# Weight halves issued in one piece, a regrouped chain, a third weight buffer and shared key tiles in a two-layer hybrid block

## The chip, the cores and the metric

The kernel runs on one core of one Trainium2 chip. The metric is the device time of one execution in microseconds (us). Engines: PE is TensorE (PEld its weight loads), DVE VectorE, ACT ScalarE, POOL GpSimd, SP SyncE. Each engine takes its instructions strictly in its own order.

## The reference

Two layers over 256 context tokens and 512 latent tokens (768 in all), model width 1024. Layer 0 keeps all 768 tokens, layer 1 gives only the 512 latent ones. All matrix products are fp32; the kernel splits each operand in two parts (hi and lo) and adds three products.

```python
# per layer: adaLN modulation, then the mixer
zc, zl = hc @ w_in, hl @ w_in          # one input projection, split into:
# A  bidirectional RWKV-7: 16 heads of 64, per token and direction
#    S = S*w - (S kk) (kk*a)^T + v k^T ;  y = S r ;  then group norm, bonus, gate
# B  GLU -> depthwise conv of width 31 -> LayerNorm -> silu
# C  grouped attention (8 query heads, 2 key heads), qk-RMSNorm, axial rotary
out = (sum_i gate_i * (branch_i @ w_branch_i)) @ w_out
x = x + mod * rms_norm(out)
# then the MLP, width 4096
x = x + mod * rms_norm(square(relu(h @ w1)) @ w2)
```

The scan of branch A is computed in chunks of 64 tokens: 12 chunks for each of two directions.

## The kernel before

**Phases.** Each layer runs rwkv_phase (branch A, the input projection and the conv; about 112 to 1370 us in layer 0, 2510 to 3690 us in layer 1), merge_phase (attention, branch products, output product) and mlp_phase (64 products by `gemm`, L389, with nothing between them).

**Pairs.** rwkv_phase goes over eight pairs of heads. One turn of the loop works on pair p and prepares pair p+1, and a generator weaver (`weave`) puts the pieces side by side. In the order of PE a turn has three stages, and this document calls them A, G and S:

- **A**, from the merge to the bonus. Of pair p: `rw_merge` (L892, its scaled copies on ACT at L900, L904), `rw_batch` (L920, L931; DVE L932, L934), then `rw_chain`, 12 steps that carry the state S (L952 and L956 give the next state, ACT scales it at L958, L968 and L970 add up the output y). Of pair p+1: the shifted inputs k, r, v (DVE L658), `rw_kk` (PE sums L717, L700, DVE L726), `rw_decay`, `rw_keys`. Of pair p-1: the readout.
- **G**, from the bonus (L877) to the last gram: `rw_grams`, twelve times eight or four small products (L810), masked by DVE (L814) and transposed by PE (L819).
- **S**, the solve: 30 DVE steps on small tiles (L861, L862) with two transposes at its end (L863, L864), small products L845 and L743, until the next merge.

**Big products.** The input projection is not a phase of its own. `job` queues products of eight k-steps; `fill(n)` takes n k-steps from the queue and issues their matmuls at L412. A k-step is three products (hi x hi, hi x lo, lo x hi), each in two pieces of 384 columns in layer 0 (one of 512 in layer 1). Four k-steps share one weight half: 24 matmuls in layer 0, 12 in layer 1. `pe(us)` calls `fill` in proportion to the small work just issued. Weight halves come by DMA, are split by ACT (`wh`, L328) and POOL (`wl`, L330) or DVE, and sit in two buffers. The 31 conv taps of each pair are DVE instructions (L473) put between the others in the same way.

**What sets the order.** Issue order gives each instruction a priority; the tile framework then orders every engine by its own estimate of when operands are ready. So a big matmul issued in one place can be moved between small ones on PE. Under `tc.high_priority()` an instruction goes ahead of those without it.

**Memory.** `KM` (values) and `BK` (keys) are separate tiles per direction; `KM` is read by L920 in A, `BK` written by `rw_keys` of the next pair in A and read by the grams in G.

Of the kernel before, what the change touches and what calls it, by code (L numbers as in the profile page):

```python
# [18 lines left out]
D = 1024  # L19
# [57 lines left out]
class Kern:  # L77
# [451 lines left out]
    def att_stats(s, T, hold):  # L529

        nc = s.nc
        rs = s.ars = s.cp.tile([128, 2, 10, 6], F32, tag="ars", name="ars", bufs=1)
        slots = []
        for n in (('BK', 0), ('BK', 1), ('KM', 0), ('KM', 1), ('GL', 0)):
            t = s.big[n]
            t = t.rearrange({3: "p a b -> p (a b)", 4: "p a b c -> p (a b c)", 5: "p a b c d -> p (a b c d)"}[len(t.shape)])
# [110 lines left out]
    def stage(s):  # L647
        return s.wp.tile([128, TOK], F32, tag="f0", name="f0", bufs=1)
# [60 lines left out]
    def rw_kk(s, P, p, I):  # L709
# [6 lines left out]
        for t in range(6):  # L716
            nc.tensor.matmul(sp[:, t, :], lhsT=sq[:, t * 128:t * 128 + 128], rhs=s.bo[:, 0:128:64], start=True, stop=True)  # L717
# [20 lines left out]
    def rw_transpose(s, src, h, dst):  # L738
# [3 lines left out]
        for m in range(6):  # L742
            nc.tensor.transpose(out=vp[:, m, :], in_=src[ROWS[h], m * 128:m * 128 + 128], identity=s.ident[ROWS[h], 64 * h:64 * h + 64])  # L743
# [45 lines left out]
    def rw_front(s, I, Q, d, g, lat):  # L789
# [18 lines left out]
        for q in range(4):  # L808
            for h in range(2):
                nc.tensor.matmul(gp[h][:, q, 0:n, :], lhsT=BK[ROWS[h], 4 * g + q].rearrange("p a b -> p (a b)"),  # L810
                                 rhs=KR[ROWS[h], 0:n, 4 * g + q, :], start=True, stop=True)
# [6 lines left out]
        for q in range(4):  # L818
            nc.tensor.transpose(out=bk[:, q].rearrange("p a b -> p (a b)"), in_=BK[:, 4 * g + q].rearrange("p a b -> p (a b)"), identity=s.ident)  # L819
# [16 lines left out]
    def rw_rest(s, d):  # L836
# [3 lines left out]
        for g, m in ((0, 8), (8, 4)):  # L840
            mv = s.g([128, 8, 64])
            for c in range(g, g + m):
                for h in range(2):
                    w = ROWS[1 - h]
                    nc.tensor.matmul(mv[ROWS[h], c - g, :], lhsT=GL[w, h, c, :], rhs=UV[w, h * 12 + c, :], start=True, stop=True)  # L845
# [20 lines left out]
    def rw_bonus(s, P, p, I, Q, T):  # L866
# [8 lines left out]
        for b, t0, t1 in s.pieces(T):  # L875
            bp = s.g([128, t1 - t0])
            nc.tensor.matmul(bp, lhsT=s.bo, rhs=ks[:, t0:t1], start=True, stop=True)  # L877
# [5 lines left out]
    def rw_merge(s, Q, d):  # L883

        nc = s.nc
# [4 lines left out]
        for q in range(12):  # L890
            for h in range(2):
                nc.tensor.matmul(xp[two[h], q, :], lhsT=GL[one[h], h, q, c:c + 32], rhs=Dn[one[h], q, :], start=True, stop=True)  # L892
        TT = Q['TT', d] = GL.rearrange("p h c t -> p (h c t)")[:, 0:768].rearrange("p (c t) -> p c t", t=64)
        Xn = Dn
        for h in range(2):
            nc.scalar.activation(out=Xn[two[h]], in_=xp[two[h]], func=AF.Copy, scale=-1.0)
        yield 1.1 + s.sched['merge']
        for h in range(2):
            for o, m in ((0, s.tlo), (32, s.thi)):
                nc.scalar.activation(out=TT[ROWS[h], :, o:o + 32], in_=Dt[ROWS[h]], func=AF.Copy, scale=m[ROWS[h]])  # L900
        tr = s.g([128, 12, 32])
# [7 lines left out]
    def rw_batch(s, Q, d, lat):  # L909
# [27 lines left out]
    def rw_chain(s, Q, lat, note, free):  # L937
# [5 lines left out]
        for k in range(NCH):  # L943
            q = (k, ORD_B[k])
            need_y = not lat or k >= 4
            seg = 0 if k < 4 else 1
            if k < NCH - 1:
                sp = s.pc.tile([128, 2, 64], F32, tag="c", name="sp")
                Sn = t("S", [128, 2, 64], 2)
                for d in range(2):  # L950
                    for h in range(2):
                        nc.tensor.matmul(sp[ROWS[h], d], lhsT=GB[d][:, h, q[d], 0, :], rhs=UV[d][:, h * 12 + q[d], :], start=d == 0, stop=d == 1 and k == 0)  # L952
                if k:
                    for d in range(2):
                        for h in range(2):
                            nc.tensor.matmul(sp[ROWS[h], d], lhsT=KR[d][ROWS[h], 0, q[d], :], rhs=S[ROWS[h], d], start=False, stop=d == 1)  # L956
                for d in range(2):
                    nc.scalar.activation(out=Sn[:, d], in_=sp[:, d], func=AF.Copy, scale=Q['lam', d][:, q[d]:q[d] + 1])  # L958
            if need_y:
                fresh = seg not in yp  # L960
                if fresh:
                    yp[seg] = s.py.tile([128, 512], F32, tag="y", name="yp")
                for part in ((1, 0) if k else (0,)):
                    for d in range(2):
                        o = (q[d] - 4 * seg) * 64
                        for h in range(2):
                            if part:
                                nc.tensor.matmul(yp[seg][ROWS[h], o:o + 64], lhsT=KR[d][ROWS[h], 1, q[d], :], rhs=S[ROWS[h], d], start=fresh, stop=False)  # L968
                            else:
                                nc.tensor.matmul(yp[seg][ROWS[h], o:o + 64], lhsT=GB[d][:, h, q[d], 1, :], rhs=UV[d][:, h * 12 + q[d], :], start=fresh, stop=d == 1 and k in (3, NCH - 1))  # L970
                        fresh = False
# [10 lines left out]
    def rw_readout(s, l, P, p, Q, T, dst):  # L982
# [144 lines left out]
    def rwkv_phase(s, l, P, T):  # L1127
# [3 lines left out]
        with ExitStack() as rc:  # L1131
# [7 lines left out]
            for a, b in lay[3]:  # L1139
# [7 lines left out]
                ('GB', [128, 2, 12, 2, 64]), ('UV', [128, 24, 64]), ('KM', [128, 12, 2, 64]))}  # L1147
# [47 lines left out]
            for p in range(8):  # L1195
# [21 lines left out]
                if more:  # L1217
                    gs.append(chain(prep(p + 1, In, Qn, *held), wait('s3'), grams(In, Qn, 0), wait('s7'), grams(In, Qn, 1), wait('s11'), grams(In, Qn, 2)))
# [16 lines left out]
            s.pin = False  # L1235
# [99 lines left out]
    def mlp_phase(s, l, PP, T, acc, actx):  # L1335
# [15 lines left out]
        with tc.tile_pool(name="mlp", bufs=1) as sp:  # L1351
# [29 lines left out]
            s.R = s.rstd(sp, ss, T, 1.0 / D, 0, CTX)  # L1381
# [65 lines left out]
```

## Time and profile before

| | us |
|---|---|
| time, median of three runs | 4514.72 (4509.4 to 4517.8) |
| the profiled execution | 4503.07, span 4501.3 |
| PE busy | 4197.0 (93%) |
| PEld busy | 3411.4 (76%) |
| DVE busy | 2642.9 (59%) |
| ACT busy | 1889.5 (42%) |
| POOL busy | 831.3 (18%) |
| mean granted clock | 0.956 of full speed |

The profiled execution is 11.65 us below the median. The busy time of PE counts a matmul until its modelled end, so matmuls that follow each other overlap in it; how long one really takes is read from the starts of its neighbours. A granted clock of 1.00 is 2.4 GHz, 0.50 is 1.2 GHz.

Stage times of a steady pair, read from the starts of L892, L877 and the end of the last L810. Pair 4 of layer 0: A 819.5 to 901.4, G to 922.5, S to 966.7. Pair 2 of layer 1: A 2953.0 to 3021.4, G to 3043.2, S to 3078.9. Sums over the seven pairs that prepare a next one: layer 0 A 543.7, G 151.8, S 324.1 us; layer 1 A 478.1, G 150.4, S 304.3 us.

### The profile page before, as it was taken

The page shows a single profiled execution, that of the slowest core. Times are in us where ns is not written, and L with a number is a line of the kernel's source. Part 1 is how long each engine was busy: PE and PEld are TensorE (multiplying, and loading weights), DVE is VectorE, ACT ScalarE, POOL GpSimd, SP SyncE. Part 2 cuts the span into 40 slices and gives each one's busy share as a digit, 9 for nine tenths or more (in the row PEclk, how much of TensorE's full clock was granted, in tenths as well). Part 3 has the DMA queues.
Part 4 walks back from the last instruction along what each step waited for, and adds up shares of the span by engine and source line. Part 5 has one row for each costly group of instructions (what it writes and reads, how often), then busy time and mean ns, then how long its engine had stood idle before and what let it go on. Part 6 is the DMA issues. An engine that isn't in the chain of part 4 may idle for free. (4 is left out here: it accounts for less than half of the span.)

```text
span 4501.3 us, 76922 instructions
## 1 busy us (share of the span) xinstructions
PE 4197.0 (93%) x31232; PEld 3411.4 (76%) x31232; DVE 2642.9 (59%) x4762; ACT 1889.5 (42%) x3690; POOL 831.3 (18%) x737
## 2 busy tenths in 40 slices
PE   6999999999998989899999899999999988898998
PEld 4888888888786668689999667877777775475886
DVE  3788788887855443132233568778787845443344
ACT  3455445444534442232223354555555534434333
POOL 0011221212112144300000102122122212262001
PEclk8999999999999999999999889999999979998998
DMA  4211111111224234343322221111111223142332
GB/s 161 62 47 53 57 58 57 51 52 58 73 84 157 71 110 142 126 141 117 107 87 63 69 61 52 50 60 47 56 54 57 75 71 121 57 133 64 96 96 82
DMA packets 438346, 364.05 MB, mean 81 GB/s; under 512 B 19022, under 2 KB 386792, under 8 KB 431848
## 3 DMA queue, kind: packets, MB, share of 16 engines
q1 hardware_dynamic: 417256, 279.43, 20.5%
q10 hardware_dynamic: 20736, 79.70, 4.9%
q8 instruction: 247, 4.05, 0.4%
q14 instruction: 107, 0.88, 0.1%
HBM read 299.29 MB, written 53.48 MB: 78 GB/s over the span
## 5 line engine op out<-in xcount | busy, mean ns | idle before, releaser
L328 ACT ACTIVATE wh<-raw 128x512 fp32r<-128x512 f32 x700 | 441.4, 631 | 1261.5 <-PE mm L389 558.3
L330 POOL TENSOR_TENSOR wl<-raw,wh 128x512 fp32r<-128x512 f32 x388 | 535.5, 1381 | 2062.3 <-ACT wh L328 1699.1
L412 PE MATMUL mm<-hh,wh 128*128 128x384 f32 (+1 forms) x2072 | 668.6, 381 | 49.4 <-ACT wh L328 40.7
L412 PE MATMUL mm<-hl,wh 128*128 128x384 f32 (+1 forms) x2072 | 644.5, 370 | 7.0 <-POOL hl L330 7.0
L412 PE MATMUL mm<-hh,wl 128*128 128x384 f32 (+1 forms) x2072 | 641.4, 369 | 4.9 <-POOL wl L330 4.6
L332 DVE TENSOR_TENSOR wl<-raw,wh 128x512 fp32r<-128x512 f32 x312 | 215.5, 691 | 589.7 <-ACT wh L328 586.4
L412 PEld LDWEIGHTS mm<-hh,wh 128*128 128x128 f32 x2072 | 379.2, 195 | 112.7 <-ACT wh L328 45.6
L473 DVE SCALAR_TENSOR_TENSOR cv<-u,dw,cv 128x783 f32<-128x783 f32 (+1 forms) x480 | 458.3, 955 | 3.1
L412 PEld LDWEIGHTS mm<-hl,wh 128*128 128x128 f32 x2072 | 389.6, 195 | 47.7 <-issue 12.1
L412 PEld LDWEIGHTS mm<-hh,wl 128*128 128x128 f32 x2072 | 388.0, 194 | 47.1 <-POOL wl L330 10.8
L412 PE MATMUL mm<-oh,wh 128*128 128x384 f32 (+1 forms) x768 | 256.7, 389 | 12.1 <-DVE acc L1273 4.1
L412 PE MATMUL mm<-oh,wl 128*128 128x384 f32 (+1 forms) x768 | 245.9, 374 | 22.0 <-POOL wl L330 22.0
L412 PE MATMUL mm<-ol,wh 128*128 128x384 f32 (+1 forms) x768 | 243.5, 370 | 6.6 <-POOL ol L330 5.6
L389 PE MATMUL mm<-hh,wh 128*128 128x384 f32 (+1 forms) x768 | 239.3, 367 | 6.3 <-ACT hh L347 3.6
L389 PE MATMUL mm<-hl,wh 128*128 128x384 f32 (+1 forms) x768 | 238.3, 365 | 5.5 <-POOL hl L330 5.0
L389 PE MATMUL mm<-hh,wl 128*128 128x384 f32 (+1 forms) x768 | 236.0, 362 | 0.0
L389 PE MATMUL mm<-fh,wh 128*128 128x384 f32 (+1 forms) x768 | 230.2, 353 | 0.0
L389 PE MATMUL mm<-fh,wl 128*128 128x384 f32 (+1 forms) x768 | 230.0, 353 | 0.0
L389 PE MATMUL mm<-fl,wh 128*128 128x384 f32 (+1 forms) x768 | 229.8, 353 | 0.0
L862 DVE TENSOR_TENSOR A<-A,Z 128x30 f32<-128x30 f32 (+14 forms) x480 | 198.2, 413 | 15.8
L861 DVE TENSOR_TENSOR Z<-A 128x30 f32<-128x30 f32 (+14 forms) x480 | 190.7, 397 | 16.5
L412 PEld LDWEIGHTS mm<-oh,wh 128*128 128x128 f32 x768 | 143.9, 195 | 55.2 <-ACT wh L328 15.8
(294 smaller groups left out, 7425.6 us busy)
## 6 DMA issues: line engine op xcount, KB each, us to landing
raw<-in_w_in_dram SPq DMA_DIRECT2D x316, 256.0 KB
raw<-in_w_ff_dram SPq DMA_DIRECT2D x256, 256.0 KB
wmod<-in_w_mod_dram ACTq DMA_DIRECT2D x48, 1024.0 KB
raw<-in_w_branch_dram SPq DMA_DIRECT2D x96, 256.0 KB
z<-f ACTq DMA_DIRECT2D x40, 384.0 KB
gt<-z SPq DMA_DIRECT2D x24, 384.0 KB
raw<-in_w_out_dram SPq DMA_DIRECT2D x32, 256.0 KB
z<-f ACTq DMA_DIRECT2D x32, 256.0 KB
```

What stands on the lines that cost most here:

```text
L328: nc.scalar.activation(out=hi, in_=src, func=AF.Copy)
L330: nc.gpsimd.tensor_tensor(out=lo, in0=src, in1=hi.bitcast(F32), op=ALU.subtract)
L332: nc.vector.tensor_tensor(out=lo, in0=src, in1=hi.bitcast(F32), op=ALU.subtract)
L389: nc.tensor.matmul(ps[:, b, :t1 - t0], lhsT=w[:, k % 4, :], rhs=a[:, t0:t1], start=k == 0 and f == 0, stop=k == KT - 1 and f == 2)
L412: ins = nc.tensor.matmul(s.jps[:, b, :t1 - t0], lhsT=w[:, k % 4, :], rhs=a[:, t0:t1], start=k == 0 and f == 0, stop=k == KT - 1 and f == 2)
L473: s.tap_pin(nc.vector.scalar_tensor_tensor(out=hold['c'], in0=u[:, k:k + L], scalar=w(k), in1=hold['c'], op0=ALU.mult, op1=ALU.add))
L861: nc.vector.tensor_tensor(out=tm, in0=X[:, k + 1:, k:k + 1].to_broadcast([128, n, k]), in1=X[:, k:k + 1, 0:k].to_broadcast([128, n, k]), o ...
L862: nc.vector.tensor_tensor(out=X[:, k + 1:, 0:k], in0=X[:, k + 1:, 0:k], in1=tm, op=ALU.add)
```

## The change

- **`fill`**: of the 24 (or 12) matmuls of a weight half all but the first are issued at high priority. A branch that never ran (`s.pin`) goes.
- **Buffers**: three weight halves in place of two, and `fill` asks for halves two ahead. The stage tile f0 of the input products gets two buffers.
- **Keys**: `KM` becomes another name for `BK`. `rw_keys` of the next pair now waits in the weaver for the batch of this pair (`b0`, `b1`). The attention's scratch slots move accordingly.
- **Merge**: the scaled copies move from ACT (four instructions on 64 rows) to DVE (two on 128 rows), per direction. The two evictions on ACT get an order-only dependency on the last weight split that was issued.
- **Chain**: y's first part (GB x UV) leads, then both parts of the state, its eviction, then y's second part.

```diff
+    def keep(s, first):
+        return nullcontext() if first else s.tc.high_priority()
...
-                while s.halves and len(s.ready) < 2:
+                while s.halves and len(s.ready) < s.nw:
...
-                    ins = nc.tensor.matmul(s.jps[:, b, :t1 - t0], lhsT=w[:, k % 4, :], rhs=a[:, t0:t1], start=k == 0 and f == 0, stop=k == KT - 1 and f == 2)
-                    if s.pin and f == 0 and b == 0:
-                        s.tc.keep_in_program_order(ins)
+                    with s.keep(k % 4 == 0 and f == 0 and b == 0):
+                        nc.tensor.matmul(s.jps[:, b, :t1 - t0], lhsT=w[:, k % 4, :], rhs=a[:, t0:t1], start=k == 0 and f == 0, stop=k == KT - 1 and f == 2)
...
-        return s.wp.tile([128, TOK], F32, tag="f0", name="f0", bufs=1)
+        return s.wp.tile([128, TOK], F32, tag="f0", name="f0", bufs=2)
...
         for h in range(2):
-            nc.scalar.activation(out=Xn[two[h]], in_=xp[two[h]], func=AF.Copy, scale=-1.0)
+            ins = nc.scalar.activation(out=Xn[two[h]], in_=xp[two[h]], func=AF.Copy, scale=-1.0)
+            s.tc.add_manual_dep(ins.ins, hi.ins.name, mybir.DependencyInfo(mybir.DependencyClass.NoSync, mybir.DependencyReason.DATA), reason="weights first")
...
-        for h in range(2):
-            for o, m in ((0, s.tlo), (32, s.thi)):
-                nc.scalar.activation(out=TT[ROWS[h], :, o:o + 32], in_=Dt[ROWS[h]], func=AF.Copy, scale=m[ROWS[h]])
+        for o, m in ((0, s.tlo), (32, s.thi)):
+            nc.vector.tensor_scalar(out=TT[:, :, o:o + 32], in0=Dt, scalar1=m, scalar2=None, op0=ALU.mult)
...
-        s.nraw, s.nw, s.lo_pool, s.turn = 2, 2, False, 0
+        s.nraw, s.nw, s.lo_pool, s.turn = 2, 3, False, 0
...
+            s.big.update({('KM', d): s.big['BK', d] for d in range(2)})
...
-                return chain(s.after(I, 'k', 0, s.rw_kk(P, p, I)), *held, s.rw_decay(P, p, Q), s.rw_keys(P, p, I, Q, 0), s.rw_keys(P, p, I, Q, 1),
+                return chain(s.after(I, 'k', 0, s.rw_kk(P, p, I)), *held, s.rw_decay(P, p, Q), wait('b0'), s.rw_keys(P, p, I, Q, 0), wait('b1'), s.rw_keys(P, p, I, Q, 1),
```

What the instruction order shows. Over the whole program the matmuls of L412 stand in 975 unbroken runs before and 386 runs now, with the same number of matmuls. Three places show where they go.

PE in stage G of pair 4 of layer 0, before. `g<-KR,BK` are grams, `g<-cst,BK` their transposes, `mm` the big products.

```order
L877 MATMUL g<-key,cst 128x384 x2
L412 MATMUL mm<-hh,wh 128x384
L412 MATMUL mm<-hl,wh 128x384
L810 MATMUL g<-KR_656,BK_655 128x128 x8
L412 MATMUL mm<-hl,wh 128x384
L412 MATMUL mm<-hh,wl 128x384
L819 MATMUL g<-cst,BK_655 128x128 x4
L412 MATMUL mm<-hh,wl 128x384
L412 MATMUL mm<-hh,wh 128x384
L810 MATMUL g<-KR_662,BK_661 128x128 x8
```

The same place now. The line of dots after the first three big rows stands for three more such triples, which complete a half of 24.

```order
L879 MATMUL g<-key,cst 128x384 x2
L417 MATMUL mm<-hh,wh 128x384 x2
L417 MATMUL mm<-hl,wh 128x384 x2
L417 MATMUL mm<-hh,wl 128x384 x2
...
L812 MATMUL g<-KR_656,BK_655 128x128 x8
L417 MATMUL mm<-hh,wh 128x384 x2
...
L821 MATMUL g<-cst,BK_655 128x128 x4
L812 MATMUL g<-KR_661,BK_660 128x128 x4
L417 MATMUL mm<-hh,wh 128x384 x2
...
```

Between bonus and last gram 34 big matmuls in 11 runs stood before; now there are 192 in 8 runs, each a whole half.

PE in the chain of the same pair, before.

```order
L968 MATMUL yp<-S,KR_656 64x64 x2
L412 MATMUL mm<-hh,wl 128x384
L952 MATMUL sp<-UV_659,GB_658 64x64 x2
L952 MATMUL sp<-UV_665,GB_664 64x64 x2
L956 MATMUL sp<-S,KR_656 64x64 x2
L956 MATMUL sp<-S,KR_662 64x64 x2
L968 MATMUL yp<-S,KR_662 64x64 x2
L970 MATMUL yp<-UV_659,GB_658 64x64 x2
L970 MATMUL yp<-UV_665,GB_664 64x64 x2
L412 MATMUL mm<-hh,wl 128x384
L412 MATMUL mm<-hh,wh 128x384
```

And now:

```order
L976 MATMUL yp<-S,KR_656 64x64 x2
L964 MATMUL sp<-UV_659,GB_658 64x64 x2
L964 MATMUL sp<-UV_664,GB_663 64x64 x2
L968 MATMUL sp<-S,KR_656 64x64 x2
L968 MATMUL sp<-S,KR_661 64x64 x2
L976 MATMUL yp<-S,KR_661 64x64 x2
L958 MATMUL yp<-UV_659,GB_658 64x64 x2
L958 MATMUL yp<-UV_664,GB_663 64x64 x2
L976 MATMUL yp<-S,KR_656 64x64 x2
```

The big matmuls that stood between the steps are gone: stage A held 175 of them in 29 runs and now holds 72 in 3 runs, all before the batch or after the last step.

PE right after the solve, before: the merge (L892), the sums of kk (L717), the second part of the merge (L904) and the broadcast for kk (L700), of which dots leave out 17 further rows of L412.

```order
L892 MATMUL g<-Z,GL_663 32x32 x24
L412 MATMUL mm<-hh,wh 128x384 x2
...
L717 MATMUL g<-cst,ksq 128x2 x6
L412 MATMUL mm<-hh,wh 128x384
...
L904 MATMUL g<-Z 32x32 x24
L412 MATMUL mm<-hh,wh 128x384
...
L700 MATMUL g<-cst,rb 128x128 x3
L920 MATMUL g<-KM_660,GL_657 64x128 x8
```

And now, where each line of dots completes one half of 24:

```order
L894 MATMUL g<-Z,GL_662 32x32 x24
L719 MATMUL g<-cst,ksq 128x2 x6
L417 MATMUL mm<-hh,wh 128x384 x2
...
L907 MATMUL g<-Z 32x32 x48
L417 MATMUL mm<-hh,wh 128x384 x2
...
L702 MATMUL g<-cst,rb 128x128 x3
L923 MATMUL g<-BK_655,GL_657 64x128 x8
```

From merge to broadcast PE passes 51 big matmuls before and 48 now. Stage S held 175 big matmuls in 12 runs and holds 120 in 5. On DVE, six of the shifted inputs' instructions (L658, two runs each for k and r into G, for v into S), two or three taps and the first tap leave stage A, and four scaled copies and three gram inputs come into it. In layer 1 the counts per pair go from about 106 / 24 / 120 in A / G / S (25, 10 and 11 runs) to about 60 / 77 / 105 (5, 4 and 6 runs). Before the first merge 624 big matmuls in 29 runs become 840 in 22 (layer 0) and 444 in 28 become 564 in 21 (layer 1); between the last merge and the attention 399 in 44 become 72 in 3, and 106 in 21 become 48 in 4. In the attention 407 in 88 become 468 in 28, and 138 in 30 become 168 in 18; the products after the attention of layer 0 fall from 1141 to 1068.

## Rows read from the trace of the kernel before

**Rows 1.** The page: busy time by engine, share of the span, instructions.

```profile
PE 4197.0 (93%) x31232; PEld 3411.4 (76%) x31232; DVE 2642.9 (59%) x4762; ACT 1889.5 (42%) x3690; POOL 831.3 (18%) x737
```

**Rows 2.** Windows, by stage: window; us, then each engine's busy time and instructions, clock.

```profile
819.50:901.40 81.90, 80.33 (x957) 65.00 (x956) 66.79 (x102) 43.91 (x103) 18.50 (x20) 0.96 0.17 54
901.40:922.50 21.10, 20.47 (x155) 17.49 (x155) 13.86 (x34) 8.15 (x16) 2.35 (x2) 1.00 0.18 63
922.50:966.70 44.20, 41.72 (x313) 37.68 (x313) 37.04 (x80) 19.35 (x35) 9.28 (x7) 0.96 0.17 47
2953.00:3021.40 68.40, 66.39 (x837) 49.52 (x836) 56.78 (x97) 43.00 (x99) 14.19 (x21) 1.00 0.16 46
3021.40:3043.20 21.80, 21.57 (x143) 17.03 (x143) 13.11 (x31) 8.36 (x18) 3.61 (x3) 1.00 0.19 63
3043.20:3078.90 35.70, 32.62 (x254) 26.63 (x254) 33.38 (x74) 14.17 (x27) 8.24 (x6) 0.99 0.25 71
```

**Rows 3.** Timeline of PE, unbroken (MLP), then broken (stage G): start, us, instruction.

```profile
2039.93 0.51 PE L389 MATMUL mm<-fh,wl 128*128 128x384 f32 x2
2040.28 0.51 PE L389 MATMUL mm<-fh,wh 128*128 128x384 f32 x2
...
913.33 0.42 PE L412 MATMUL mm<-hh,wh 128*128 128x384 f32 x1
913.59 0.34 PE L412 MATMUL mm<-hl,wh 128*128 128x384 f32 x1
913.85 1.88 PE L810 MATMUL g<-KR,BK 64*128 64x128 f32 x16
```

**Rows 4.** Waits of DVE in stage A of pair 4: total, times, longest.

```profile
DVE in_kk L726 <- PE g L700: 6.3, 1, 6.3
DVE in_r L658 <- ACT in_r L655: 3.1, 1, 3.1
```

**Rows 5.** Lines of DVE, stages A to S of pair 4: count, busy, mean ns, idle before.

```profile
L473 DVE SCALAR_TENSOR_TENSOR cv<-u,dw,cv 128x783 f32<-128x783 f32 x30 | 30.8, 1027 | 0.1
L658 DVE SCALAR_TENSOR_TENSOR in_v<-f,H,in_v 128x255 f32<-128x255 f32 (+1 forms) x4 | 3.5, 867 | 0.0
L658 DVE SCALAR_TENSOR_TENSOR in_r<-f,H,in_r 128x255 f32<-128x255 f32 (+1 forms) x4 | 2.2, 612 | 3.1 <-ACT in_r L655 3.1
L831 DVE TENSOR_SCALAR Z<-GL 32x384 f32<-32x384 f32 x4 | 2.4, 594 | 0.0
L803 DVE TENSOR_TENSOR KR<-in_kk,KR 128x256 f32<-128x256 f32 x6 | 2.5, 414 | 0.0
```

**Rows 6.** Timeline of PE in the chain of layer 0's last pair.

```profile
1316.76 0.45 PE L952 MATMUL sp<-UV,GB 128*64 128x64 f32 x8
1318.14 0.44 PE L412 MATMUL mm<-hh,wh 128*128 128x384 f32 x1
```

**Rows 7.** Windows of layer 1 and 0: a wait, what follows it, two chain stretches.

```profile
3605.00:3607.30 2.30, 0.05 (x1) 0.00 (x0) 2.30 (x5) 0.63 (x1) 1.20 (x1) 1.00 0.42 116
3607.40:3624.50 17.10, 10.41 (x202) 8.32 (x202) 8.13 (x15) 8.39 (x16) 0.50 (x1) 0.50 0.11 33
3648.40:3689.30 40.90, 40.90 (x310) 35.08 (x307) 9.68 (x41) 5.06 (x17) 1.28 (x1) 0.50 0.04 14
859.70:866.50 6.80, 6.80 (x108) 5.62 (x107) 5.01 (x8) 3.80 (x12) 1.48 (x3) 1.00 0.32 99
```

**Rows 8.** Timeline of PE in layer 1's last chain, at half clock.

```profile
3686.65 0.70 PE L952 MATMUL sp<-UV,GB 128*64 128x64 f32 x8
3688.95 0.67 PE L412 MATMUL mm<-hh,wh 128*128 128x512 f32 x1
```

**Rows 9.** Waits of PE, and of ACT, over the whole span.

```profile
PE mm L412 <- ACT wh L328: 43.8, 15, 7.9
PE mm L412 <- POOL wl L330: 26.6, 21, 4.6
ACT wh L328 <- PE mm L412: 483.0, 194, 10.8
```

More of the change, by code (lines that the diff above doesn't have):

```diff
@@ L1 @@
-from contextlib import ExitStack
+from contextlib import ExitStack, nullcontext
 import numpy as np
@@ L327, in split @@
         nc = s.nc
-        nc.scalar.activation(out=hi, in_=src, func=AF.Copy)
+        s.last_hi = nc.scalar.activation(out=hi, in_=src, func=AF.Copy)
         if pool:
@@ L533, in att_stats @@
         slots = []
-        for n in (('BK', 0), ('BK', 1), ('KM', 0), ('KM', 1), ('GL', 0)):
-            t = s.big[n]
-            t = t.rearrange({3: "p a b -> p (a b)", 4: "p a b c -> p (a b c)", 5: "p a b c d -> p (a b c d)"}[len(t.shape)])
+        for t in [s.big[n, d] for n in ('BK', 'GL') for d in range(2)] + [s.A]:
+            t = t.rearrange({2: "p a -> p a", 4: "p a b c -> p (a b c)"}[len(t.shape)])
             slots += [t[:, c:c + TOK] for c in range(0, t.shape[1], TOK)]
@@ L716, in rw_kk @@
         for t in range(6):
-            nc.tensor.matmul(sp[:, t, :], lhsT=sq[:, t * 128:t * 128 + 128], rhs=s.bo[:, 0:128:64], start=True, stop=True)
+            s.nc.tensor.matmul(sp[:, t, :], lhsT=sq[:, t * 128:t * 128 + 128], rhs=s.bo[:, 0:128:64], start=True, stop=True)
         yield 1.2 + s.sched['sums']
@@ L876, in rw_bonus @@
             bp = s.g([128, t1 - t0])
-            nc.tensor.matmul(bp, lhsT=s.bo, rhs=ks[:, t0:t1], start=True, stop=True)
+            s.nc.tensor.matmul(bp, lhsT=s.bo, rhs=ks[:, t0:t1], start=True, stop=True)
             nc.vector.tensor_tensor(out=bv[:, t0:t1], in0=I['v'][:, t0:t1], in1=bp, op=ALU.mult)
@@ L883, in rw_merge @@
     def rw_merge(s, Q, d):
-        nc = s.nc
+        nc, hi = s.nc, s.last_hi
         GL = s.big['GL', d]
@@ L891, in rw_merge @@
             for h in range(2):
-                nc.tensor.matmul(xp[two[h], q, :], lhsT=GL[one[h], h, q, c:c + 32], rhs=Dn[one[h], q, :], start=True, stop=True)
+                s.nc.tensor.matmul(xp[two[h], q, :], lhsT=GL[one[h], h, q, c:c + 32], rhs=Dn[one[h], q, :], start=True, stop=True)
         TT = Q['TT', d] = GL.rearrange("p h c t -> p (h c t)")[:, 0:768].rearrange("p (c t) -> p c t", t=64)
@@ L903, in rw_merge @@
             for h in range(2):
-                nc.tensor.matmul(tr[one[h], q, :], lhsT=Xn[two[h], q, :], rhs=Dt[two[h], q, :], start=True, stop=True)
+                s.nc.tensor.matmul(tr[one[h], q, :], lhsT=Xn[two[h], q, :], rhs=Dt[two[h], q, :], start=True, stop=True)
         for h in range(2):
@@ L946, in rw_chain @@
             seg = 0 if k < 4 else 1
+            if need_y:
+                fresh = seg not in yp
+                if fresh:
+                    yp[seg] = s.py.tile([128, 512], F32, tag="y", name="yp")
+                for d in range(2):
+                    o = (q[d] - 4 * seg) * 64
+                    for h in range(2):
+                        s.nc.tensor.matmul(yp[seg][ROWS[h], o:o + 64], lhsT=GB[d][:, h, q[d], 1, :], rhs=UV[d][:, h * 12 + q[d], :], start=fresh and d == 0, stop=False)
             if k < NCH - 1:
@@ L951, in rw_chain @@
                     for h in range(2):
[L952 to L956, printed above, removed]
+                        s.nc.tensor.matmul(sp[ROWS[h], d], lhsT=GB[d][:, h, q[d], 0, :], rhs=UV[d][:, h * 12 + q[d], :], start=d == 0, stop=d == 1 and k == 0)
+            if k and k < NCH - 1:
+                for d in range(2):
+                    for h in range(2):
+                        s.nc.tensor.matmul(sp[ROWS[h], d], lhsT=KR[d][ROWS[h], 0, q[d], :], rhs=S[ROWS[h], d], start=False, stop=d == 1)
+            if k < NCH - 1:
                 for d in range(2):
                     nc.scalar.activation(out=Sn[:, d], in_=sp[:, d], func=AF.Copy, scale=Q['lam', d][:, q[d]:q[d] + 1])
[L959 to L971, printed above, removed]
+            if need_y and k:
+                for d in range(2):
+                    o = (q[d] - 4 * seg) * 64
+                    for h in range(2):
+                        s.nc.tensor.matmul(yp[seg][ROWS[h], o:o + 64], lhsT=KR[d][ROWS[h], 1, q[d], :], rhs=S[ROWS[h], d], start=False, stop=d == 1 and k in (3, NCH - 1))
             S = Sn
@@ L1015, in rw_readout @@
             gp = s.g([128, t1 - t0])
-            nc.tensor.matmul(gp, lhsT=Q['g2'], rhs=s.sgd[:, t0:t1], start=True, stop=True)
+            s.nc.tensor.matmul(gp, lhsT=Q['g2'], rhs=s.sgd[:, t0:t1], start=True, stop=True)
             nc.vector.tensor_tensor(out=y[:, t0:t1], in0=y[:, t0:t1], in1=gp, op=ALU.mult)
@@ L1217, in rwkv_phase @@
                 if more:
-                    gs.append(chain(prep(p + 1, In, Qn, *held), wait('s3'), grams(In, Qn, 0), wait('s7'), grams(In, Qn, 1), wait('s11'), grams(In, Qn, 2)))
+                    gs.append(chain(prep(p + 1, In, Qn, wait, *held), wait('s3'), grams(In, Qn, 0), wait('s7'), grams(In, Qn, 1), wait('s11'), grams(In, Qn, 2)))
                 else:
```

26 lines of the change are left out of this document (12 added, 14 removed).

## The prediction

> **What bounds the kernel now.** I read the page first: PE is busy 93% of the span, DVE 59%, ACT 42% [rows 1]. That alone says that the sum of PE's work sets the time. Then the windows by stage, since the stages of a pair have different limits [rows 2]. In layer 0, A has PE at 80.3 of 81.9 us and DVE at 66.8; G has PE at 20.5 of 21.1 and DVE at only 13.9; S has PE at 41.7 of 44.2 and DVE at 37.0. In layer 1, S is already DVE's: 33.4 of 35.7 against PE's 32.6. So DVE stands close behind PE in A and S, and far behind in G. PE is the bound because big products are spread so that both engines stay busy; whoever moves them between stages shifts the bound.
>
> The Trainium skill (Perfetto Trace Analysis, section Identifying the Most-Contended Engine) warns that matmul busy share is no measure of how near PE is to its limit and that the weight loads' share is better. In A of layer 0 that share is 65.0 of 81.9 [rows 2], so by the page a fifth of A would be PE time to win; the next paragraph prices that from rows.
>
> **What a break costs.** In the MLP two big matmuls start 0.35 us after the two before them, 0.174 each [rows 3]. In G a run of two, between transposes and grams, takes from 913.33 to 913.85, 0.26 each: 0.085 more for each, and I allow as much (an estimate) for the small matmul ahead: 0.26 us for each break. The order has 975 runs before and 386 now, so 589 breaks go: 153 us, if PE stayed the bound everywhere. A matmul of 512 columns I take as 0.232 (0.174 x 512/384).
>
> **Stage G.** Before, 21.1 us hold 34 big matmuls (5.9) in 11 runs (2.9), which leaves 12.3 for the small ones [rows 2]. Now 192 in 8 runs stand there: 12.3 + 33.4 + 2.1 = 47.8. PE arrives from stage A after waits, so I add 2 us for a slow start (see the clock, below): 50. DVE has some 24 us of work in it and doesn't decide. Seven pairs: 350 against 151.8, +198. In layer 1 the mean is 21.5, less 24 x 0.232 and 10 x 0.26, so 13.3 of small work; now 77 x 0.232 + 5 x 0.26 = 19.2 on top: 32.5, seven times 228 against 150.4, +77. This is PE's own order and the firmest term.
>
> **Stage S.** PE in layer 0 falls from 175 matmuls to 120, from 41.7 to about 30, so the 37.0 us of DVE [rows 2] decide, plus 3.5 of L658 for v [rows 5] that come in and less some 2 that leave: about 39 with its gaps. 273 against 324.1: -51. In layer 1: 37 each, 259 against 304.3: -45.
>
> **Stage A.** PE has 80.3 - 175 x 0.174 - 29 x 0.26 = 42.3 us of small work [rows 2] and now 72 x 0.174 + 3 x 0.26 = 13.3 of big: 55.6. So DVE decides. Its 66.8 lose L658 for k, r and v (2.2 + 2.2 + 3.5, k priced as r) and three taps at 1.03; they gain four scaled copies, for which the nearest row is L831 at 0.59 (2.4), and three gram inputs at 0.41 (1.2) [rows 5]: 59.5. To that come its waits, 15.1 us before (81.9 less 66.8) [rows 2]. The L658 part (3.1 for r [rows 4]) leaves with the inputs. The largest, 6.3 for kk's broadcast [rows 4], stays: the order has 48 big matmuls between merge and broadcast where 51 stood, but in two closed halves, with kk's sums and the second part of the merge between them. PE needs 8.4 us for these, some 5 for the small products and their evictions, and up to 4 more if the first half runs at half clock after the wait for the solve; DVE has about 8 us to do meanwhile. That is a wait of about 9, and with 5 for the small ones 14: A = 73. Bounds: 60, if nothing waits, and 82, if nothing is won. 7 x 73 = 511 against 543.7: -33. In layer 1 the same steps give 56.8 [rows 2] less 6 = 51, and 11 of waits (its own 11.6 today): 62, bounds 51 to 72; 434 against 478.1: -44.
>
> The other edits of A sit inside these numbers. The keys that now wait for the batch (KM on BK): behind L772 on DVE stand all later keys and the bonus; the batch needs the same merge that DVE has already waited for, so I count nothing, and up to 5 us a pair if the batch is late (within the 82). The evictions that queue behind the last weight split: the split itself has waited up to 10.8 us for a buffer [rows 9]; the third buffer takes that wait away in most cases, so nothing, with 0.6 us a split as the near bound and 10.8 a merge as the far one. The copies that leave ACT free an engine that is busy 44 of 82 us [rows 2]: nothing. The regrouped chain: one unfilled step takes 1.38 us from L952 to the next product [rows 6], PE work in either order; nothing.
>
> **Outside the steady pairs.** Matmuls moved and breaks saved, each at the prices above: before the first merge +36 (layer 0) and +26 (layer 1); last pairs -68 and -18, of which I give back 20 since their chains then have nothing to fill their own gaps; attention -5 and +4; after it -13. Together about -20 after rounding. PE's waits for weight halves are 43.8 + 26.6 us [rows 9]; the third buffer can take between none and all of them; most fall where products already stand unbroken and ACT's or POOL's rate decides, so I take -15.
>
> **Sum.** Layer 0: -33 + 198 - 51 = +114. Layer 1: -44 + 77 - 45 = -12. Outside -20, weights -15. +67 us. On the profiled 4503.07 that is 4570; the median of the runs shown lies 11.65 above its profiled run, so 4582, which I give as 4580. In short: the products gather in G, where DVE has little to do, and are missing in A and S, where DVE then stands alone.
>
> **The clock.** After PE has sat through the wait for the solve (3605.00 to 3607.30, busy 0.05 us) it runs at half clock for the next 17 us, and the chain at 3648.4 to 3689.3, nearly all small matmuls, is at half clock for 40.9 us though PE shows no gap; the chain stretch at 859.7 has small matmuls too and full clock [rows 7]. A step at half clock takes 2.30 us [rows 8] against 1.38 [rows 6], 1.67 times. The Trainium skill (TensorE: Matmul & The Clock Gate, section HAM oscillation) says that work blocks shorter than the waits between them can each start cold. It speaks against a chain emptied of big products, and the first two rows agree; the third doesn't.
>
> **Rivals.**
> 1. *PE stays the bound, breaks are won (faster).* For it: PE at 98% of A. Against: DVE's 37.0 in S leaves at most 5 to 7 us there. If A waited for nothing (60 and 51), the sum is 67 - 13 x 7 - 11 x 7 = -101, time about 4415; with half of these waits gone, -17 and 4500. Even the full 153 us would give 4360. It decides if DVE finds kk's broadcast ready when it comes, that is if PE finishes the two halves within 8 us of the solve's end.
> 2. *The emptied chain runs at half clock in both layers (much slower).* In A of layer 0 the 42.3 us of small work become 71, with the big 84, +11 on 73; in layer 1 35.6 (66.4 less 24.6 and 6.2) become 59, with 14 of big 74, +12 on 62; G starts slower by 3. 7 x 29 = +200, time about 4780; if only layer 1 does so, +100 and 4680. For it: the row at 3648; against: the row at 859.
> 3. *Nothing but the order on paper.* Terms cancel within 0.2%, about 9 us, which is what a measurement of this kernel tells from no change. It needs A's waits to shrink by some 60 us in all.
> That halves aren't kept whole I rule out: the order shows runs of 24 and 12.
>
> **Chances.** Forecast with A between 66 and 80 (4515 to 4640): 0.50. Clock case, in part or whole (over 4640): 0.18. Waits of A partly gone (4430 to 4505): 0.20; nearly all breaks won (under 4430): 0.07. No change: 0.05. So faster 0.27, same 0.05, slower 0.68. The range 4440 to 4690 leaves out the two far cases; the forecast's own is 4515 to 4640.
>
> **What would show it.** G of layer 0 near 50 us, PE busy, DVE near half; S near 39 with DVE busy over 90%; A near 73 with DVE's wait for L702 at 9 us or so. Fewer half-clock slices than before in layer 1 would speak against rival 2. I am wrong if G stays near 30, or if A falls to 60.

## The result, and the profile after

| | us |
|---|---|
| before, median of 4 | 4515.36 (4509.4 to 4517.8) |
| changed, median of 3 | 4733.12 (4730.1 to 4747.2) |
| ratio | 1.0493 (95%: 1.0464 to 1.0521) |
| forecast | 4580 (4440 to 4690) |

The change makes the kernel 4.9% slower. The direction was forecast; the size was not: 218 us by the medians where 67 were expected, and the time lies outside the range. A fourth run of the changed kernel took 5337.83 us at a mean clock of 0.714; median and ratio leave it out (with it the median is 4740.17).

The profiled execution has a span of 4745.4 us, 244 more than before; it is the slowest of the three. The page's busy times:

```profile
PE 4274.4 (90%) x31232; PEld 3547.8 (75%) x31232; DVE 2632.9 (55%) x4828; ACT 1814.5 (38%) x3562; POOL 807.5 (17%) x735
```

PE is busy 77 us longer than before with the same number of matmuls [rows 1], though 589 breaks are gone. The clock points the same way: its mean is 0.911 in place of 0.956, and added up over the clock records PE spends 849 us at half clock, before 394.

The stages, as windows of the changed kernel: A, G, S of pair 4 of layer 0, then of pair 2 of layer 1. The columns: window; us; busy us of PE, PEld, DVE, ACT and POOL, each with its instructions; granted clock; DMA share and GB/s.

```profile
921.30:1008.30 87.00, 75.51 (x853) 60.14 (x854) 61.93 (x100) 35.40 (x90) 6.03 (x14) 0.72 0.07 23
1008.30:1056.10 47.80, 47.77 (x314) 44.35 (x312) 22.15 (x46) 17.26 (x30) 11.86 (x9) 1.00 0.20 61
1056.10:1091.70 35.60, 28.49 (x259) 26.43 (x259) 33.37 (x76) 14.44 (x26) 6.78 (x5) 0.96 0.27 78
3137.60:3201.80 64.20, 56.44 (x768) 42.62 (x768) 50.36 (x89) 34.20 (x85) 10.34 (x16) 0.90 0.11 33
3201.80:3238.20 36.40, 36.37 (x191) 31.21 (x191) 17.26 (x37) 12.31 (x24) 4.36 (x4) 0.76 0.12 37
3238.20:3279.50 41.30, 32.79 (x259) 27.17 (x260) 38.73 (x80) 16.59 (x31) 11.54 (x9) 0.93 0.27 80
```

In layer 0, G is PE's at full clock (47.77 of 47.80) and S is DVE's (33.37 of 35.60). A is the surprise: 103 big matmuls have left it, and it takes 87.0 us where it took 81.9, at a clock of 0.72 where it had 0.96. Over the seven pairs of each layer and the rest of the span (from the starts of L894 and L879, the last L812 and the span):

| | before | forecast | after | half clock before, after |
|---|---|---|---|---|
| layer 0: A | 543.7 | 511 | 573.7 | 7, 238 |
| G | 151.8 | 350 | 334.8 | 0, 4 |
| S | 324.1 | 273 | 247.2 | 20, 17 |
| layer 1: A | 478.1 | 434 | 471.6 | 57, 96 |
| G | 150.4 | 228 | 263.6 | 0, 116 |
| S | 304.3 | 259 | 273.6 | 31, 35 |
| all the rest | 2549 | 2514 | 2581 | 279, 343 |

Half clock in A of layer 0 stands mostly where big matmuls are missing: pairs 0 and 1, which hold 120 and 144 of them, have 6 and 13 us of it, the four pairs with 72 have 43 to 48; but pair 5, with 120, has 38.

Where the half clock begins in A, and what the chain looks like there. First the window of such a stretch in pair 3 of layer 0, and the part of it without a wait; then PE's timeline inside that part:

```profile
802.40:836.50 34.10, 29.65 (x238) 21.23 (x239) 25.03 (x27) 16.90 (x41) 2.90 (x10) 0.50 0.08 28
807.20:827.80 20.60, 20.60 (x214) 14.48 (x214) 13.95 (x15) 10.88 (x31) 1.99 (x8) 0.50 0.08 26
```

```profile
822.53 0.69 PE L964 MATMUL sp<-UV,GB 128*64 128x64 f32 x8
823.15 0.69 PE L968 MATMUL sp<-S,KR 64*64 64x64 f32 x8
823.64 0.43 PE L976 MATMUL yp<-S,KR 64*64 64x64 f32 x4
823.99 0.69 PE L958 MATMUL yp<-UV,GB 128*64 128x64 f32 x8
824.61 0.48 PE L976 MATMUL yp<-S,KR 64*64 64x64 f32 x4
825.02 0.69 PE L964 MATMUL sp<-UV,GB 128*64 128x64 f32 x8
```

A step takes 2.49 us (822.53 to 825.02), near the 2.30 of the half-clock chain before [rows 8] and not the 1.38 of [rows 6]. PE has no gap from 807.20 to 827.80: it is busy, but 208 of its 214 matmuls there have 64 columns. Just before the clock falls at 802.40, PE ran small products with waits between them, the last two of 0.79 and 0.67 us; big matmuls are back from 831.24 on, and the clock is full again at 836.50. ACT scales the state of each step (its evictions, L971), and other ACT work stands between these evictions. ACT and DVE in the same microseconds:

```profile
823.96 0.52 ACT L971 ACTIVATE S<-sp,lam 128x64 f32<-128x64 f32 x2 [0.73 <-PE sp L968]
826.17 0.41 ACT L800 ACTIVATE KR<-sg 128x252 f32<-128x252 f32 x1 [1.70 <-PE sp L968]
826.49 0.50 ACT L971 ACTIVATE S<-sp,lam 128x64 f32<-128x64 f32 x2
...
827.96 0.58 ACT L983 ACTIVATE y<-yp 128x512 f32<-128x512 f32 x1
828.43 0.83 ACT L777 ACTIVATE Z<-A 128x768 f32<-128x768 f32 x1
```

```profile
824.13 0.42 DVE L805 TENSOR_TENSOR KR<-in_kk,KR 128x256 f32<-128x256 f32 x1
829.30 1.92 DVE L784 TENSOR_TENSOR BK<-BK,Z 64x768 f32<-64x768 f32 x2 [4.75 <-ACT Z L777]
```

DVE waits 4.75 us for L777, which waits for nothing of its own: it stands on ACT behind a copy into KR (L800) that waits 1.70 us for PE's slow chain, behind the next state's evictions, and behind that of the output (L983). So the keys of the next pair, work of DVE, run at the chain's pace. DVE's waits in A of pair 4, the counterpart of [rows 4] (total, times, longest):

```profile
DVE in_kk L728 <- PE g L702: 9.5, 1, 9.5
...
DVE BK L774 <- ACT A L770: 4.0, 1, 4.0
DVE BK L784 <- ACT Z L777: 3.2, 1, 3.2
```

PE's waits over the span, the counterpart of [rows 9]:

```profile
PE g L894 <- DVE Z L865: 96.6, 16, 9.5
PE g L879 <- DVE key L873: 57.1, 10, 8.3
...
PE mm L417 <- ACT cv L458: 20.2, 6, 3.4
...
PE mm L417 <- ACT wh L328: 3.8, 3, 2.9
PE mm L417 <- POOL wl L330: 3.2, 6, 1.1
```

Before, the first two were:

```profile
PE g L892 <- DVE Z L863: 21.5, 4, 9.0
PE g L877 <- DVE key L871: 15.5, 7, 6.4
```

The waits for weight halves are nearly gone, 70.4 to 7.0 us. Three others are new or grown: for the solve (L894), where S has too few big products to cover DVE; for the bonus (L879), after which PE runs the first 17 us of layer 1's G at half clock; and for the conv tile (L458). The stretch after the second wait, in pair 2 of layer 1:

```profile
3198.60:3219.00 20.40, 17.17 (x70) 14.54 (x71) 13.02 (x28) 4.06 (x8) 0.00 (x0) 0.50 0.07 27
```

### The profile page after: what moved, and what is told of

It reads as the page before. It is cut to its first block, busy times and chain, and to the rows that moved or that the text cites. A ratio compares the mean times of both kernels' runs of the same rounds, so it can differ in the third digit from the quotient of the medians.

```text
span 4745.4 us, 76977 instructions
## 1 busy us (share of the span) xinstructions
PE 4274.4 (90%) x31232; PEld 3547.8 (75%) x31232; DVE 2632.9 (55%) x4828; ACT 1814.5 (38%) x3562; POOL 807.5 (17%) x735
## 5 line engine op out<-in xcount | busy, mean ns | idle before, releaser
L328 ACT ACTIVATE wh<-raw 128x512 fp32r<-128x512 f32 x700 | 441.2, 631 | 1644.9 <-PE mm L389 564.8
L330 POOL TENSOR_TENSOR wl<-raw,wh 128x512 fp32r<-128x512 f32 x386 | 517.0, 1340 | 1954.9 <-ACT wh L328 1543.2
L417 PE MATMUL mm<-hh,wh 128*128 128x384 f32 (+1 forms) x2072 | 658.2, 382 | 28.8 <-ACT cv L458 20.2
L417 PE MATMUL mm<-hl,wh 128*128 128x384 f32 (+1 forms) x2072 | 622.7, 365 | 6.5 <-POOL hl L330 6.5
L417 PE MATMUL mm<-hh,wl 128*128 128x384 f32 (+1 forms) x2072 | 619.1, 363 | 0.0
L417 PEld LDWEIGHTS mm<-hh,wh 128*128 128x128 f32 x2072 | 390.4, 200 | 77.4 <-ACT cv L458 21.2
L417 PEld LDWEIGHTS mm<-hl,wh 128*128 128x128 f32 x2072 | 401.3, 199 | 27.2 <-POOL hl L330 9.0
L417 PEld LDWEIGHTS mm<-hh,wl 128*128 128x128 f32 x2072 | 399.8, 198 | 24.6 <-DVE wl L332 1.9
L816 DVE TENSOR_TENSOR GL<-g,masks 128x256 f32<-128x256 f32 x192 | 80.7, 421 | 310.9 <-PE g L812 310.6
L389 PE MATMUL mm<-hh,wh 128*128 128x384 f32 (+1 forms) x768 | 238.3, 365 | 6.3 <-ACT hh L347 3.6
L389 PE MATMUL mm<-hl,wh 128*128 128x384 f32 (+1 forms) x768 | 236.8, 363 | 5.8 <-POOL hl L330 5.4
L389 PE MATMUL mm<-hh,wl 128*128 128x384 f32 (+1 forms) x768 | 234.8, 361 | 0.0
L863 DVE TENSOR_TENSOR Z<-A 128x30 f32<-128x30 f32 (+14 forms) x480 | 217.9, 454 | 15.9
L812 PEld LDWEIGHTS g<-KR,BK 64*128 64x128 f32 x1536 | 173.1, 216 | 41.2 <-issue 35.8
```

The source lines that it names most:

```text
L328: s.last_hi = nc.scalar.activation(out=hi, in_=src, func=AF.Copy)
L389: nc.tensor.matmul(ps[:, b, :t1 - t0], lhsT=w[:, k % 4, :], rhs=a[:, t0:t1], start=k == 0 and f == 0, stop=k == KT - 1 and f == 2)
L812: s.nc.tensor.matmul(gp[h][:, q, 0:n, :], lhsT=BK[ROWS[h], 4 * g + q].rearrange("p a b -> p (a b)"), rhs=KR[ROWS[h], 0:n, 4 * g + q, :], s ...
L816: nc.vector.tensor_tensor(out=G, in0=gp[h][:, :, x, :], in1=s.mask(d, h, x).unsqueeze(1).to_broadcast([128, 4, 64]), op=ALU.mult)
L863: nc.vector.tensor_tensor(out=tm, in0=X[:, k + 1:, k:k + 1].to_broadcast([128, n, k]), in1=X[:, k:k + 1, 0:k].to_broadcast([128, n, k]), o ...
```

## The experiments

All ratios are to the kernel before, timed on the same chip, with 95% intervals.

**e1: the priority taken away.**

```diff
-        return nullcontext() if first else s.tc.high_priority()
+        return nullcontext()
```

> The changed kernel with all big matmuls at normal priority again; third weight buffer, shared key tiles, merge copies on DVE, queued evictions and regrouped chain stay. Theory H (the closed halves empty the chain and the solve of big products and pile them up in the grams): the order has 936 runs again and 175 / 34 / 175 matmuls in A / G / S, so the stages return to about 80 / 21 / 46 us in layer 0 and the time to 4480 to 4540. Rival M (the shared key tiles, the merge's copies or the queued evictions make A late): half or more of the loss stays, 4640 or more.

4442.17 us, 0.9845 (0.9829 to 0.9861). A, G, S of layer 0 are back at 549.1, 146.4 and 301.5. The whole loss, and more, is the closed halves; the other edits together win 1.5%, which neither theory gave. M falls.

**e2: the closed halves alone, in the kernel before.**

```diff
-                    ins = nc.tensor.matmul(s.jps[:, b, :t1 - t0], ...)
...
+                    with (nullcontext() if k % 4 == 0 and f == 0 and b == 0 else s.tc.high_priority()):
+                        nc.tensor.matmul(s.jps[:, b, :t1 - t0], ...)
```

> The kernel before with nothing but the closed halves (two weight buffers, own KM tiles, merge and chain as before). H: A, G, S of layer 0 near 84, 48, 36 us and 4680 to 4790. M: near the kernel before, 4500 to 4560. If the third buffer was what softened the closed halves, above 4790.

4729.98 us, 1.0483 (1.0465 to 1.05); A 577.3, G 294.9, S 257.5 in layer 0. The same loss from the other side. With closed halves, then, the other edits win nothing that shows.

**e3 and e7: more PE work in the chain, to warm it.** e3 adds one fp32 product of 256 columns that waits for each step's state, e7 two products of the big kind.

```diff
+            if k:
+                with s.tc.high_priority():
+                    warm = s.g([128, 256])
+                    s.nc.tensor.matmul(warm, lhsT=S.rearrange("p a b -> p (a b)"), rhs=s.sgd[:, 256:512], start=True, stop=True)
```

```diff
-                sp = s.pc.tile([128, 2, 64], F32, tag="c", name="sp")
+                spw = s.pc.tile([128, 512], F32, tag="c", name="sp")
+                sp = spw[:, 0:128].rearrange("p (a b) -> p a b", b=64)
+                with s.tc.high_priority():
+                    for i in range(2):
+                        s.nc.tensor.matmul(spw[:, 128:512], lhsT=s.hh[:, i, 0:128], rhs=s.hh[:, i, 0:384], start=True, stop=True)
```

> The changed kernel with one extra matmul (128x256, result unread) in each chain step, which waits for that step's state: about 0.45 us at full clock, 11 a pair, 166 in the program, 75 us of added work. Theory C (the emptied chain drops PE to half clock, and that is what makes A long in layer 0): the half-clock stretch of some 34 us in A of layer 0 goes, A falls from 84 to 74-80 in spite of the added work, time 4660 to 4730. Rival D (A is long since DVE and the round trips of the chain are, whatever the clock): all or most of the added work shows, 4780 to 4830.

> The changed kernel with two extra big matmuls (128x384 of the product's own kind, result unread) at the start of each chain step, 11 a pair, 176 steps in all: about 0.6 us a step at full clock with its seams, 100 us of added work. Theory C (the clock of the emptied chain makes A long): half clock in A of layer 0 falls from 238 us to under 80, A from 574 to under 560 in spite of 46 us of added work, time 4690 to 4760. Rival D (DVE's busy time and waits make A long, whatever the clock): half clock falls as well, but A stays at 570 or grows, 4770 to 4850.

e3: 4771.56, 1.0575 (1.0559 to 1.0591). Half clock in A of layer 0 falls from 238 to 164 us, A grows from 573.7 to 588.7: between the two theories. e7: 4794.5, 1.061 (1.0577 to 1.0642). Half clock stays at 229 and A grows by 45.6 us, as much as the 46 added; but four of the seven pairs also hold one half more in A, so not all of it is the fillers'. The fillers did not hold the clock up, so they are no test of what it is worth. But e7 shows something else: in A of layer 0 little of the work added to PE is covered. A of pair 4 in e7, with 72 big matmuls as in the changed kernel:

```profile
937.60:1031.50 93.90, 83.74 (x875) 64.95 (x876) 64.52 (x108) 35.46 (x90) 6.46 (x14) 0.73 0.08 24
```

PE has 8.2 us more busy time there than in the changed kernel's A, DVE 2.6, and the stage is 6.9 longer. In layer 1 the same fillers make the seven A only 11 us longer, with 38 us less half clock.

What the clock is worth in A can be read from e3's own trace. Here are A of pairs 3 and 4 of its layer 1, with the same matmuls and DVE's busy time within 0.4 us; 11.2 and 38.2 us of them are at half clock:

```profile
3301.60:3364.60 63.00, 58.08 (x764) 42.50 (x764) 49.67 (x89) 32.11 (x79) 8.36 (x13) 0.91 0.09 26
3438.40:3510.40 72.00, 69.14 (x765) 48.98 (x765) 50.02 (x89) 32.11 (x79) 6.38 (x13) 0.73 0.08 23
```

So 27 us more at half clock make A 9 us longer; in e11 below, between pairs 2 and 3 of layer 1, 27 us make it 6 longer. By these two, the 33 us that half clock grew by in each A of layer 0 are worth some 7 to 11 us (an estimate, carried over from layer 1).

**e10: less PE work in the chain.**

```diff
-            if need_y and k:
+            if need_y and k in (3, NCH - 1):
```

> The changed kernel without the second part of y (KR x S) except in steps 3 and 11, so the output is not the reference's: nine steps of a pair lose four small matmuls, 0.33 us at full and 0.57 at half clock. Theory P (PE's own chain sets the end of A): 3 to 5 us less a pair, 4660 to 4700. Theory D (DVE and its waits on ACT set it): at most 1 us a pair, 4720 to 4745.

4680.04 us, 1.0375 (1.0355 to 1.0395). A of layer 0 falls by 27.5 us, 3.9 a pair, and half clock in it from 238 to 156, so part of the fall can be the clock's. A of pair 4, which falls most (12.5 us), with 72 big matmuls and DVE's busy time as in the changed kernel within 0.4 us:

```profile
916.10:990.60 74.50, 61.46 (x781) 50.67 (x782) 61.53 (x98) 35.36 (x90) 10.22 (x14) 0.84 0.08 26
```

P holds for layer 0: PE's chain sets the end of A, not DVE. In layer 1 A falls by only 1.5 us a pair, with 31 us more half clock over the seven.

**e4, e6: shorter units.** One k-step (6 or 3 matmuls) and two k-steps (12 or 6) in place of four.

```diff
-                    with s.keep(k % 4 == 0 and f == 0 and b == 0):
+                    with s.keep(f == 0 and b == 0):
```

```diff
-                    with s.keep(k % 4 == 0 and f == 0 and b == 0):
+                    with s.keep(k % 2 == 0 and f == 0 and b == 0):
```

> The changed kernel with a unit of one k-step (6 or 3 matmuls unbroken) in place of a half (24 or 12). The order has 703 runs in place of 386 and 186 / 60 / 140 matmuls in A / G / S of layer 0. H: the stages have their mix back and 233 breaks of 0.26 us are still saved against the kernel before, 4440 to 4520. Rival (any priority of big over small products delays the small ones): 4580 or more.

> The changed kernel with a unit of two k-steps (12 or 6 matmuls), 537 runs. It holds about 170 / 80 / 145 matmuls in A / G / S of layer 0. H: between one k-step (4407) and the closed half (4740), nearer to the former since A keeps its products, 4400 to 4500. If the length of the run itself (the wait of a small product behind it) is what costs, half way, 4550 to 4600.

e4: 4407.25 us, 0.9765 (0.9746 to 0.9783), the fastest of all and below what H gave. e6: 4496.35, 0.9963 (0.9951 to 0.9976). Layer 0 of the two: A 564.7 and 564.8, G 169.7 and 208.3, S 277.5 and 277.5. A, G, S of pair 4 in e4:

```profile
792.70:879.20 86.50, 82.11 (x967) 68.41 (x967) 70.83 (x111) 43.50 (x101) 15.70 (x20) 0.94 0.15 48
879.20:903.00 23.80, 23.57 (x189) 20.26 (x187) 12.57 (x33) 10.08 (x19) 4.55 (x3) 1.00 0.25 77
903.00:939.70 36.70, 30.29 (x270) 28.01 (x271) 34.58 (x80) 15.91 (x28) 8.15 (x6) 0.96 0.18 54
```

This A holds 186 big matmuls and lasts 86.5 us; the changed kernel's holds 72 and lasts 87.0; over the seven pairs A takes 564.7 and 573.7. What leaves A earns nothing there, and costs in G.

**e5, e8: closed halves only outside the pairs that prepare a next one.** Inside them normal priority (e5) or units of one k-step (e8).

```diff
-        return nullcontext() if first else s.tc.high_priority()
+        return nullcontext() if first or s.loose else s.tc.high_priority()
...
-                more = p < 7
+                more = s.loose = p < 7
```

```diff
-                    with s.keep(k % 4 == 0 and f == 0 and b == 0):
+                    with s.keep((s.loose or k % 4 == 0) and f == 0 and b == 0):
...
-                more = p < 7
+                more = s.loose = p < 7
```

> The changed kernel with the closed halves only outside the pairs that prepare a next one; inside them the big products have normal priority. Theory H (the loss is made inside the pairs, where closed halves empty A and fill G): 4400 to 4450, at or below e1, as PE is the bound outside and 147 of e1's 936 breaks go. Rival O (closed halves also cost outside, where small products wait for them): 4460 or more, above e1.

> The changed kernel with units of one k-step inside the pairs that prepare a next one and closed halves elsewhere. H: e4's stages in the pairs and 84 breaks less outside, at 0.26 us some 20 us: 4380 to 4410, at or below e4. Rival O: above 4415.

e5: 4499.16, 0.9965 (0.9949 to 0.9981), 57 us above e1. e8: 4545.12, 1.0066 (1.0051 to 1.0081), 138 above e4. O holds, H falls here: outside the pairs closed halves cost too. In e8 the seven pairs take 1012.3 and 914.8 us, as in e4 (1011.6 and 909.8); it loses before the first merge (262.6 against 226.7 and, in layer 1, 208.6 against 180.2), in the last pairs (117.8 against 97.8, 79.9 against 69.3) and around the attention (+10 and +14). Products that move ahead of the first merge (786 big matmuls stand there in e8, 624 in e4) lengthen that stretch, and the pairs that they leave don't get shorter.

**e9, e12: what wins in e1.** e1 with two weight buffers, and e1 with the chain of the kernel before.

```diff
-        s.nraw, s.nw, s.lo_pool, s.turn = 2, 3, False, 0
+        s.nraw, s.nw, s.lo_pool, s.turn = 2, 2, False, 0
```

```diff
-            if need_y:
-                fresh = seg not in yp
...
+            if need_y:
+                fresh = seg not in yp
...
+                for part in ((1, 0) if k else (0,)):
...
```

> e1 (the changed kernel, all big products at normal priority) with two weight buffers in place of three. Theory W (what e1 wins on the kernel before, 70 us, is PE's waits for weight halves, 43.8 + 26.6 us, that the third buffer takes away): 4490 to 4530, the waits back at 55 to 80 us. Rival (the chain's order, the merge's copies on DVE and the second stage tile win it): 4440 to 4460.

> e1 (the changed kernel, all big products at normal priority) with the chain of the kernel before. e9 left 40 us of e1's gain unexplained, 20 of them in the pairs of layer 0. Theory R (the regrouped chain wins them: y's first part leads and covers the wait for the state): 4460 to 4485. Rival (the copies on DVE or the second stage tile win them): 4435 to 4455.

e9: 4470.25, 0.9911 (0.9886 to 0.9935); e12: 4447.09, 0.9856 (0.9836 to 0.9877). So of e1's gain the third buffer has 28 us, most of it around layer 0's attention (555.5 to 538.6), and the regrouped chain nothing that can be told from zero. Two buffers bring back only part of the waits, 29.5 us where e1 has 5.7. PE's waits for weights, in e9:

```profile
PE mm L417 <- POOL wl L330: 22.2, 13, 4.5
PE mm L417 <- ACT wh L328: 7.3, 4, 3.7
```

W was half right. The other 40 us belong to the merge's copies, the queued evictions, the shared keys or the second stage tile; which of them was not tried.

**e11: a second buffer for the conv's tile.**

```diff
-            hold['c'] = s.rp.tile([128, L], F32, tag="cv", name="cv")
+            hold['c'] = s.rp.tile([128, L], F32, tag="cv", name="cv", bufs=2)
```

> The changed kernel with two buffers for the conv's tile cv. Theory B (the queue of closed halves stands still in the chain because its next product is a conv product, whose eviction to cv waits for the taps of the pair before): one half a pair goes back from G to A (96 / 168 in place of 72 / 192), PE's wait for L458 (20.2 us, six times) goes, G of layer 0 falls by 4 us a pair, 4690 to 4720. Rival: the half in A makes A longer by as much, 4735 to 4745.

4703.84 us, 1.0429 (1.0409 to 1.0449). The wait for L458 is gone, one half a pair moves from G to A, G of layer 0 falls from 334.8 to 307.5, 3.9 a pair, and A stays (571.3). Elsewhere in the pairs half of that is lost again: S of layer 0 grows by 9 us, and in layer 1 half clock leaves G (116 to 16) and comes up in A (96 to 198), which grows by 16 while S falls by 10. B holds, for one half a pair, which fits this picture: under priority the products run as early as their buffers let them, until the next in the queue is one whose result has no place yet; there all wait, and then they come together.

## Why the prediction was right and wrong

- **G and S of layer 0: right.** G was forecast at 50 a pair and took 47.8, which is the sum without the 2 us for a slow start; S was forecast at 39 and took 35.3, so it won 77 us where 51 were forecast. That G is PE's own order and S DVE's could be read from the order and the rows.
- **The wait for kk's broadcast: right.** About 9 us forecast, 9.5 measured in pair 4, 9.2 to 10.1 in six of the seven pairs.
- **A of layer 0: wrong, +30 in place of -33.** The step that failed is "PE has 80.3 - 175 x 0.174 - 29 x 0.26 = 42.3 us of small work [rows 2] and now 72 x 0.174 + 3 x 0.26 = 13.3 of big: 55.6. So DVE decides." PE was busy 75.5 us in that stage, not 55.6: the small work was priced at full clock, and 238 of the 574 us of A ran at half clock. DVE's busy time came out near the forecast (61.9 against 59.5). e10 showed that PE's chain sets the end, and by the estimate from e3 and e11 the half clock is worth the 9 us a pair that were missed.
- **The clock was rival 2's, and its chance was too small.** Its price for layer 0 (+11 a pair) comes near: A came out at 82.0 a pair where the forecast had 73. That is in part luck. The price has all the small work at half clock, PE busy for 84 us and no waits; measured are half clock in 34 of the 82 us, PE busy for 73.3 (the mean of the seven pairs) and idle for 8.7. For layer 1 it gave A 74; A took 67.4, and more of the half clock fell on G, after the wait for the bonus. The row that I held against rival 2, 859.7 to 866.5 [rows 7], was a weak witness, as it is not a bare chain: over half of it is the batch's products of 128 columns, and big matmuls end 0.3 us before it.

```profile
L931 PE MATMUL g<-GB,KM 64*64 64x128 f32 x60 | 4.0, 274 | 0.0
```

- **A of layer 1: too low by 38.** It was forecast at 62 a pair, from the matmul counts of a steady pair. Pairs 2, 3, 4 and 6, with 48 big matmuls, take 63.4 to 65.2; pairs 0, 1 and 5 hold 72 to 120 and take 67.6 to 76.1. S of layer 1 took 39 a pair where 37 were forecast.
- **G of layer 1: direction right, too small by 36.** The mean was forecast at 32.5 a pair and took 37.7, with 17 of them at half clock. I had added a slow start in layer 0, where there was none, and none in layer 1. What it costs shows in G of pair 4 of layer 1, first in e7, then in the changed kernel: the same 191 matmuls, at full clock after a wait for the bonus of 1.1 us in e7, and with 15 us at half clock after one of 6.0 in the changed kernel.

```profile
3534.80:3563.80 29.00, 28.96 (x191) 24.99 (x191) 14.87 (x35) 12.44 (x24) 4.99 (x5) 1.00 0.15 47
3486.90:3522.50 35.60, 35.60 (x191) 30.45 (x191) 15.02 (x35) 12.31 (x24) 4.37 (x4) 0.78 0.12 38
```

- **Outside the pairs: +32 in place of -35.** The terms before the first merges were right (+36 and +26 forecast, +37 and +23 measured). The last pairs were forecast at -66 and gave -21: their 86.2 us in layer 0 hold 43 at half clock. The third buffer took 63 us of waits where I had counted 15, but next to closed halves that does not show in the time: e2, with two buffers, lost as much (1.0483 against 1.0493).
- **Rival 1 (breaks are won)** is not wrong in kind: e4 saves 272 of the 975 breaks, keeps its mix and is 2.4% faster. But e1, which saves 39, is already 1.5% faster, 28 us of it by the third buffer (e9); what e4 wins beyond e1 is 35 us for 233 breaks, 0.15 each and not 0.26.

The Trainium skill's page TensorE: Matmul & The Clock Gate, section HAM oscillation, speaks of short work blocks with waits between them. Layer 1's G, at half clock after a wait for the bonus of 5.7 to 8.3 us in six of its seven pairs, agrees. The chain of layer 0 does not fit: it stays at half clock for 20.6 us in which PE shows no wait. What keeps the clock down there stays open; two kinds of filler did not settle it.

## What to carry to other kernels

A break between small and big matmuls has a price (0.26 us by the rows before, 0.15 by e4 against e1), but so has the place of the big ones: they are worth most where the other engine is long, and a stage that loses them need not get shorter. Before closing runs, count per stage what the order does, and price the small work that is left alone at the lower clock as well. Choose the unit by trial between the ends: 6 matmuls gave 4407 us, 12 gave 4496, 24 gave 4733, and none closed 4442.

## What the runs showed of the hardware

In A of pair 3 of layer 0, PE ran at half clock for 34.1 us (busy 29.65). For 20.6 of these it showed no wait (busy 20.60), with 208 of 214 matmuls of 64 columns. Two added big matmuls in each step left the half clock of that stage as it was (229 in place of 238 us over seven pairs). Before the change, with big matmuls between the steps, the same seven stages had 7 us of it.

The same matmuls took 63.0 us in one stage A of e3 and 72.0 in another, with 27 us more at half clock; in G of layer 1 they took 29.0 us at full clock and 35.6 with 15 us at half clock.
